# A depthwise convolution's banded tiles built in zeroed buffers, and an FFN weight ring split in two

## The chip, the cores and the metric

One core of a Trainium2 chip runs the program. The metric is the time of one execution on the device, in microseconds (us). Five engines work beside each other, each in its own fixed order of instructions: TensorE (PE, matmuls, with its weight loads as PEld), VectorE (DVE), ScalarE (ACT), GpSimd (POOL) and SyncE (SP). Transfers are issued from the queues of SP, ACT and POOL.

## The reference

One layer of a hybrid encoder block in float32: D = 1024, 2048 positions and 16 meta positions ahead of them.

```python
h = concatenate([meta, x])
z = rms_norm(h, norm_mix_g)
conv_v, conv_gate, ssm_u = split(z @ w_in)              # 512 channels each
u = conv_v * sigmoid(conv_gate)
y = depthwise_conv(u, conv_w, width=31, centred) + conv_b
conv_out = silu(layer_norm(y, ln_g, ln_b))
y5 = gelu(bidirectional_ssm(ssm_u) + d_skip * ssm_u)    # 32 groups of 16 channels
ssm_out = y5 * sigmoid(y5 @ glu_w + glu_b)
h = h + concatenate([conv_out, ssm_out]) @ w_out
z = rms_norm(h, norm_ffn_g)
h = h + square(relu(z @ w_ff1)) @ w_ff2                 # 4096 wide
return rms_norm(h, norm_final_g)[16:]
```

The change bears on `depthwise_conv` and on the buffers of the two big products behind it.

## The kernel before

Float32 products are made of three matmuls on a high and a low part (`mm3`, L158 to L160); `split` makes the parts, the high one by a cast on ACT (L141) and the low one by a subtraction on DVE (L142). A matmul of 512 columns follows the one ahead of it after 0.23 us. A scheduler sets each engine's order when the program is built; pools with rings of buffers put in the waits.

The stages around the change:

- **Parameters, near 90 us.** `conv_params` turns the 31 taps of each channel round, puts them into a row `wp` of 63 with zeros on both sides, and multiplies that row by an 8-channel diagonal to `ep`, [128, 504], which is stored in `edr[j]` in DRAM (j counts 128 channels).
- **Projections, to 496 us.** The gate and value products end with v(3,3). `stv` is value times gate; POOL stores it in `vdr` (L282). It is laid out so that 16 steps of time lie on one partition row.
- **Convolution, 496 to 595 us.** Sixteen calls of `conv_quad`, 32 channels each. A call loads `u8` (a piece of `vdr`), and for each of four groups of 8 channels a tile `cb` of 128 rows by 384 columns (16 steps x 8 channels, by 3 x 128): the tap of the right distance where row and column have the same channel, else 0. Three matmuls per group (L910, each in two records) with `u8` as the stationary operand sum into PSUM; four adds on DVE put the bias to it and write `cv[blk]`. The tiles `cb` lie in a ring of six, each filled by one transfer from `edr` with 128 runs of 1536 bytes (L908), 192 KB.
- **Beside and behind it.** `load_wout(0)` and `load_wout(1)` bring the two halves of w_out through three `raw4` buffers (L924) and split them to woh/wol. `s5_out(blk)` loads `y` (L958), makes GELU of it and splits the result to `ghl`, multiplies by the GLU weights (`glu`, from `gw`), and hands `mhl` to `wout_mm(0, blk, ...)` (`wo0_t`, products of w_out's lower half). `ln_out` normalises `cv` for `wout_mm(1, blk, ...)`. glu0 and wo0_0 to wo0_3 belong to block 0, glu1 and wo0_4 and so on to block 1.
- **Slots.** `zslot` gives out four large buffers, two with the tag za and two with zb. They held z, its blocks in turn, then w_out's halves, then FFN operands (zx1, zx6 in za; zx3, zx4 and every second chunk of hid and w2 in zb).
- **FFN, 840 us on.** Seven products per pair of 128-wide pieces (a Strassen step). `hid_pair` makes the weight operands 1, 2, 6, 7, 5, 3, 4 in that order, each a tile [128, 2, 4, 128] of a ring of nine with the tag w.

Of the kernel before, what the change touches and what calls it, by code (L numbers as in the profile page):

```python
# [37 lines left out]
def hymba_kernel(ctx, tc, x, meta, norm_mix_g, w_in, conv_w, conv_b, conv_ln_g, conv_ln_b,  # L38
# [70 lines left out]
    edr = [DR.tile([P, 504], F32, name=f"edr{j}") for j in range(4)]  # L109
# [52 lines left out]
    with ExitStack() as es2:  # L162
# [181 lines left out]
        with (tc.tile_pool(name="pp", bufs=1, reuse_waits="tile") as PP,  # L344
# [254 lines left out]
            def conv_params():  # L599
                cw = tp([31, 512], "cw", tag="cw", bufs=2)  # L600
                SP.dma_start(cw, conv_w[0])
                m8 = tp([P, 8], "m8")
                V.tensor_reduce(out=m8, in_=ident.rearrange("p (a c) -> p c a", c=8), axis=mybir.AxisListType.X,
                                op=ALU.add)
                for j in range(4):
# [5 lines left out]
                    ep = tp([P, 63, 8], f"ep{j}", tag="cw", bufs=2)  # L611
                    mul(ep, wp.unsqueeze(2).broadcast_to([P, 63, 8]), m8.unsqueeze(1).broadcast_to([P, 63, 8]))
                    SP.dma_start(edr[j], ep.rearrange("p i c -> p (i c)"))
# [204 lines left out]
        def z_open(half):  # L818
            for q in "12675":
                n = f"zx{q}_{half}"  # L820
                zx[q] = (zslot([P, 2, 4, 512], n, tag="za") if q in "16" else
                         PR.tile([P, 2, 4, 512], F32R, tag=f"zx{q}", name=n, bufs=1))
# [44 lines left out]
        def z_late(half):  # L867
            for q, src in zip("34", sdr[half]):
                n = f"zx{q}_{half}"
                zx[q] = zslot([P, 2, 4, 512], n, tag="zb")  # L870
# [9 lines left out]
        with tc.tile_pool(name="p3", bufs=1, reuse_waits="tile") as P3:  # L880
# [18 lines left out]
            def conv_quad(q):  # L899

                j = q // 4
                ps = ks_ps(f"cv{q}", [P, 4, NT, 8])
                u8 = t3([P, 4, W], f"u8_{q}", bufs=2, tag="u8", pool=P3R)
                SP.dma_start(u8, dap(vdr[j], (q % 4) * 32 * NT * W, [[W, P], [P * W, 4], [1, W]]))
                for i in range(4):
                    g8 = 4 * (q % 4) + i
                    cb = t3([P, 384], f"cb{q}_{i}", tag="cb", bufs=6, pool=P3R)
                    SP.dma_start(cb, dap(edr[j], g8 * 8 * 504, [[504, 8], [8, 16], [1, 384]]))  # L908
                    for m in range(3):
                        T.matmul(ps[:, i].rearrange("p t c -> p (t c)"), u8[:, i, 2 - m:2 - m + P], cb[:, ts(m, P)],  # L910
                                 start=(m == 0), stop=(m == 2))
                bv = convb[:, 32 * q:32 * q + 32].rearrange("p (i c) -> p i c", c=8).unsqueeze(2)
                for blk in range(4):
                    o = cv[blk][:, :, 32 * q:32 * q + 32].rearrange("p t (i c) -> p i t c", c=8)
                    add(o, ps[:, :, 4 * blk:4 * blk + 4, :], bv.broadcast_to([P, 4, 4, 8]))
# [3 lines left out]
            def load_wout(top):  # L919
                hi = zslot([P, 4, D], f"woh{top}")  # L920
                lo = zslot([P, 4, D], f"wol{top}")
# [121 lines left out]
    def hid_pair(p, half, P4, order, late=None):  # L1043
# [10 lines left out]
        def wsplit(q, src):  # L1054
            w[q] = P4.tile([P, 2, 4, P], F32R, tag="w", name=f"w{q}_{n}", bufs=9)
            split(w[q][:, 0], w[q][:, 1], src)
# [65 lines left out]
    def second(half, P5, chunks):  # L1122
        def bufs(c):
            if c % 2 == 0:
                return [zslot([P, 2, 2, D], f"{q}{half}_{c}", tag="zb") for q in ("hid", "w2")]
# [102 lines left out]
```

## Time and profile before

| | us |
|---|---|
| median of 3 runs (lowest, highest) | 2204.61 (2204.16, 2206.48) |
| the profiled execution, its own time | 2203.35 |
| its span in the profile | 2201.5 |
| PE busy | 2073.1 (94%) |
| DVE busy | 1541.0 (70%) |
| ACT, POOL busy | 710.4 (32%), 155.5 (7%) |
| mean granted clock of TensorE | 0.986 of full speed |

The profile shows one execution. Busy time is the union of an engine's instructions; in the rows further down, what stands in brackets or behind the bar as idle is time in which that engine stood still before the instruction, with what released it. The chain of waits goes back from the last instruction, step by step, to whatever released it. Matmuls overlap, so the length of one record (0.4 us) is more than the spacing.

### The profile page before, as it was taken

Reading aid. Unit: us, or ns where it says so; the run is one execution under the profiler, and the core shown is the slowest. Engines: PE = TensorE matmul, PEld = TensorE weight load, DVE = VectorE, ACT = ScalarE, POOL = GpSimd, SP = SyncE. Lnnn points to the kernel's source line nnn. Section 1 sums busy time; section 2 is a strip of 40 time slices with the busy share of each in tenths; the row PEclk is TensorE's granted clock in tenths of the full one; section 3 lists DMA queues with packets and bytes.
Section 4 is the critical chain, followed back from the end, with each engine's and each line's share of the span. In section 5 each row is a group of like instructions: output and inputs, shape, how many; then the busy total and the mean of one; then the engine's idle time right before and its main releaser. Section 6 shows DMA issues by size and latency. Waiting matters only on the chain.

```text
span 2201.5 us, 27237 instructions
## 1 busy us (share of the span) xinstructions
PE 2073.1 (94%) x10124; PEld 1688.7 (77%) x10124; DVE 1541.0 (70%) x2783; ACT 710.4 (32%) x1046; POOL 155.5 (7%) x240
## 2 busy tenths in 40 slices
PE   7989889896899989999999999997999999999997
PEld 5767777775687767888888888885888888888886
DVE  7866799952397388556658888868666656676767
ACT  5323222220134144444434222214444443121212
POOL 1031244500001110000000000000000000000000
PEclk9999999999999999999999999998999999999999
DMA  6245444336653566333335343434333335232322
GB/s 193 94 159 184 126 112 118 116 96 192 206 168 111 191 216 206 114 115 115 107 113 201 106 124 105 162 97 144 115 107 103 100 122 186 92 109 84 115 77 86
DMA packets 217997, 290.94 MB, mean 132 GB/s; under 512 B 22221, under 2 KB 164057, under 8 KB 217352
## 3 DMA queue, kind: packets, MB, share of 16 engines
q1 hardware_dynamic: 193512, 241.84, 35.1%
q10 hardware_dynamic: 23072, 43.10, 5.4%
q0 software_dynamic: 1280, 4.26, 0.5%
q8 instruction: 80, 1.31, 0.3%
q14 instruction: 53, 0.43, 0.1%
HBM read 206.40 MB, written 82.76 MB: 131 GB/s over the span
## 4 chain that ended last, share of the span: by engine, by line
PE 73%; DVE 11%; DMA 8%; issue 2%; ACT 1%; SPq 0%; ACTq 0%; POOL 0%; DVEq 0%; POOLq 0%
PE f L158 10%; PE f L160 10%; PE f L159 10%; PE ps L1085 9%; PE ps L1084 9%; PE ps L1083 9%; DMA cb<-edr 3%; PE wo L158 2%; PE wo L160 2%; PE wo L159 2%; DMA h<-hdr 1%; DVE zo L761 1%; DVE s L45 1%; DVE zo L760 1%; PE cv L910 1%
## 5 line engine op out<-in xcount | busy, mean ns | idle before, releaser
L45 DVE TENSOR_TENSOR acc<-acc,f 128x512 f32<-128x512 f32 x496 | 331.6, 684 | 140.2 <-PE f L160 139.6
L158 PE MATMUL f<-w,hid 128*128 128x512 f32 x1024 | 399.8, 390 | 0.5 <-DVE acc L45 0.3
L159 PE MATMUL f<-w,hid 128*128 128x512 f32 x1024 | 398.6, 389 | 0.0
L160 PE MATMUL f<-w,hid 128*128 128x512 f32 x1024 | 398.5, 389 | 0.0
L1083 PE MATMUL ps<-zx,w 128*128 128x512 f32 x896 | 353.9, 395 | 16.0 <-ACT w L141 16.0
L1085 PE MATMUL ps<-zx,w 128*128 128x512 f32 x896 | 353.7, 395 | 1.9 <-DVE w L142 1.9
L1084 PE MATMUL ps<-zx,w 128*128 128x512 f32 x896 | 354.1, 395 | 0.0
L158 PEld LDWEIGHTS f<-w,hid 128*128 128x128 f32 x1024 | 192.2, 188 | 42.2 <-DVE acc L45 2.9
L160 PEld LDWEIGHTS f<-w,hid 128*128 128x128 f32 x1024 | 192.2, 188 | 40.2
L159 PEld LDWEIGHTS f<-w,hid 128*128 128x128 f32 x1024 | 192.2, 188 | 39.6
L1083 PEld LDWEIGHTS ps<-zx,w 128*128 128x128 f32 x896 | 169.3, 189 | 56.8 <-ACT w L141 17.8
L1085 PEld LDWEIGHTS ps<-zx,w 128*128 128x128 f32 x896 | 169.4, 189 | 40.8 <-DVE w L142 2.2
L1084 PEld LDWEIGHTS ps<-zx,w 128*128 128x128 f32 x896 | 169.3, 189 | 38.6
L141 ACT CAST hid<-rawh 128x1024 fp32r<-128x1024 f32 x64 | 67.3, 1052 | 358.9 <-PE f L160 351.0
L142 DVE TENSOR_TENSOR w<-sm,w 128x512 fp32r<-128x512 f32 x128 | 87.5, 691 | 84.7 <-ACT w L141 84.7
L141 ACT CAST w<-sm 128x512 fp32r<-128x512 f32 x128 | 78.2, 618 | 158.5 <-PE ps L1085 146.6
L141 ACT CAST w<-r 128x512 fp32r<-128x512 f32 x96 | 58.8, 617 | 129.3 <-PE ps L1085 118.1
L141 ACT CAST w<-raww 128x1024 fp32r<-128x1024 f32 x64 | 67.2, 1051 | 90.5 <-DMA raww<-in_w_ff_dram 90.5
L142 DVE TENSOR_TENSOR hid<-rawh,hid 128x1024 fp32r<-128x1024 f32 x64 | 78.2, 1222 | 16.8 <-ACT hid L141 16.8
L142 DVE TENSOR_TENSOR w<-raww,w 128x1024 fp32r<-128x1024 f32 x64 | 78.1, 1220 | 10.9 <-ACT w L141 10.9
L910 PE MATMUL cv<-cb,u 128*128 128x128 f32 x384 | 60.7, 299 | 23.4 <-DMA cb<-edr 21.4
L910 PEld LDWEIGHTS cv<-cb,u 128*128 128x128 f32 x384 | 49.9, 199 | 38.1 <-issue 16.9
(301 smaller groups left out, 3373.7 us busy)
## 6 DMA issues: line engine op xcount, KB each, us to landing
r<-in_w_ff_dram SPq DMA_DIRECT2D x64, 512.0 KB
fdr<-hh ACTq DMA_DIRECT2D x64, 512.0 KB
rawh<-fdr SPq DMA_DIRECT2D x64, 512.0 KB
raww<-in_w_ff_dram SPq DMA_DIRECT2D x64, 512.0 KB
h<-hdr SPq DMA_DIRECT2D x32, 512.0 KB
cb<-edr SPq DMA_DIRECT2D x64, 192.0 KB
x<-in_x_dram SPq DMA_DIRECT2D x16, 512.0 KB
mt<-gdr SPq DMA_DIRECT2D x64, 128.0 KB
```

The source lines that it names most:

```text
L45: return V.tensor_tensor(out=o, in0=a, in1=b, op=op)
L141: S.copy(out=hi, in_=src)
L142: on.tensor_tensor(lo, src, hi.bitcast(F32), ALU.subtract)
L158: T.matmul(ps, lh, rh, start=first, stop=False)
L159: T.matmul(ps, lh, rl, start=False, stop=False)
L160: T.matmul(ps, ll, rh, start=False, stop=last)
L760: V.tensor_tensor_scan(zo[0:64, 2:4 * W + 2], f(rh)[0:64, :], f(zi)[0:64, :], 0.0, ALU.mult, ALU.add)
L761: V.tensor_tensor_scan(zo[64:128, 0:4 * W][:, ::-1], f(rh)[64:128, ::-1], f(zi)[64:128, ::-1], 0.0, ALU.mult, ALU.add)
L910: T.matmul(ps[:, i].rearrange("p t c -> p (t c)"), u8[:, i, 2 - m:2 - m + P], cb[:, ts(m, P)], start=(m == 0), stop=(m == 2))
L1083: T.matmul(ps[q], w[q][:, 0, k], z[:, 0, k, :], start=(k == 0), stop=False)
L1084: T.matmul(ps[q], w[q][:, 0, k], z[:, 1, k, :], start=False, stop=False)
L1085: T.matmul(ps[q], w[q][:, 1, k], z[:, 0, k, :], start=False, stop=(k == 3))
```

## The change

It has three parts.

1. The taps are stored as they are: `edr[j]` is [128, 63], and the multiplication by the diagonal goes.
2. `toeplitz(h)` makes one tile for two quads (eight groups of 8 channels), [128, 8, 8, 48]: 128 rows (16 steps of time for each of 8 channels) by 8 groups, 8 channels and 48 columns. Four tiles cb0 to cb3 lie in the z slots. Each is cleared once (DVE clears cb0 and cb2, POOL cb1 and cb3), and then only its diagonal blocks are filled: 8 transfers, one a channel, of 16 rows by 8 by 48, that is 128 runs of 192 bytes, 24 KB. For h from 4 on, cb0 and cb1 are filled anew in turn; what lies off the diagonal stays zero. The matmuls read 8 x 16 columns out of it with a stride of 48, PSUM has channel before time, and the adds turn that round. The ring of `cb` goes. w_out's halves and the FFN's tiles change between za and zb.
3. The ring of nine in `hid_pair` becomes one of six (products 1, 2, 6, 7) and one of three (5, 3, 4).

```diff
@@ -106,7 +106,7 @@
     ydr = [DR.tile([P, NT, P], F32, name=f"ydr{j}") for j in range(4)]
     kdr = [DR.tile([P, 4, NPK], F32, name=f"kdr{i}") for i in range(4)]
     gdr = [DR.tile([2, H, 34 * H], F32, name=f"gdr{b}") for b in range(16)]
-    edr = [DR.tile([P, 504], F32, name=f"edr{j}") for j in range(4)]
+    edr = [DR.tile([P, 63], F32, name=f"edr{j}") for j in range(4)]
     pdr = [DR.tile([P, D], F32, name=f"pdr{t}") for t in range(NT)]
     hdr = [DR.tile([P, D], F32, name=f"hdr{t}") for t in range(NT)]
     sdr = [[DR.tile([P, 4, 512], F32, name=f"sdr{half}_{q}") for q in range(2)] for half in range(2)]
@@ -599,18 +599,13 @@
             def conv_params():
                 cw = tp([31, 512], "cw", tag="cw", bufs=2)
                 SP.dma_start(cw, conv_w[0])
-                m8 = tp([P, 8], "m8")
-                V.tensor_reduce(out=m8, in_=ident.rearrange("p (a c) -> p c a", c=8), axis=mybir.AxisListType.X,
-                                op=ALU.add)
                 for j in range(4):
                     ps = tr_ps(f"tr_cw{j}")
                     T.transpose(ps[:, 0:31], cw[:, ts(j, P)], ident[0:31, 0:31])
                     wp = tp([P, 63], f"wp{j}", tag="wp", bufs=2)
                     GP.memset(wp, 0.0)
                     V.tensor_copy(wp[:, 16:47], ps[:, 0:31][:, ::-1])
-                    ep = tp([P, 63, 8], f"ep{j}", tag="cw", bufs=2)
-                    mul(ep, wp.unsqueeze(2).broadcast_to([P, 63, 8]), m8.unsqueeze(1).broadcast_to([P, 63, 8]))
-                    SP.dma_start(edr[j], ep.rearrange("p i c -> p (i c)"))
+                    SP.dma_start(edr[j], wp)
 
             z_block(0)
             z_tiles(0, 0, 2, lambda: SP.dma_start(gmix, norm_mix_g[0].partition_broadcast(P)))
@@ -818,7 +813,7 @@
         def z_open(half):
             for q in "12675":
                 n = f"zx{q}_{half}"
-                zx[q] = (zslot([P, 2, 4, 512], n, tag="za") if q in "16" else
+                zx[q] = (zslot([P, 2, 4, 512], n, tag="zb") if q in "16" else
                          PR.tile([P, 2, 4, 512], F32R, tag=f"zx{q}", name=n, bufs=1))
 
         def z_step(half, i, psa, psb, tmp):
@@ -867,7 +862,7 @@
         def z_late(half):
             for q, src in zip("34", sdr[half]):
                 n = f"zx{q}_{half}"
-                zx[q] = zslot([P, 2, 4, 512], n, tag="zb")
+                zx[q] = zslot([P, 2, 4, 512], n, tag="za")
                 for k in range(2):
                     r = (raw4 if k else lambda s_, n_: xx_tile(n_).rearrange("p (k n) -> p k n", k=2))(
                         [P, 2, 512], f"raw_{n}_{k}")
@@ -899,26 +894,38 @@
             def conv_quad(q):
 
                 j = q // 4
-                ps = ks_ps(f"cv{q}", [P, 4, NT, 8])
+                ps = ks_ps(f"cv{q}", [P, 4, 8, NT])
                 u8 = t3([P, 4, W], f"u8_{q}", bufs=2, tag="u8", pool=P3R)
                 SP.dma_start(u8, dap(vdr[j], (q % 4) * 32 * NT * W, [[W, P], [P * W, 4], [1, W]]))
+                cb = toeplitz(q // 2) if q % 2 == 0 else cbs[q // 2 if q < 8 else q // 2 % 2]
                 for i in range(4):
-                    g8 = 4 * (q % 4) + i
-                    cb = t3([P, 384], f"cb{q}_{i}", tag="cb", bufs=6, pool=P3R)
-                    SP.dma_start(cb, dap(edr[j], g8 * 8 * 504, [[504, 8], [8, 16], [1, 384]]))
                     for m in range(3):
-                        T.matmul(ps[:, i].rearrange("p t c -> p (t c)"), u8[:, i, 2 - m:2 - m + P], cb[:, ts(m, P)],
+                        T.matmul(ps[:, i], u8[:, i, 2 - m:2 - m + P], cb[:, 4 * (q % 2) + i, :, ts(m, 16)],
                                  start=(m == 0), stop=(m == 2))
                 bv = convb[:, 32 * q:32 * q + 32].rearrange("p (i c) -> p i c", c=8).unsqueeze(2)
                 for blk in range(4):
                     o = cv[blk][:, :, 32 * q:32 * q + 32].rearrange("p t (i c) -> p i t c", c=8)
-                    add(o, ps[:, :, 4 * blk:4 * blk + 4, :], bv.broadcast_to([P, 4, 4, 8]))
+                    add(o, ps[:, :, :, 4 * blk:4 * blk + 4].rearrange("p i c t -> p i t c"),
+                        bv.broadcast_to([P, 4, 4, 8]))
+
+            cbs = []
+
+            def toeplitz(h):
+
+                n = h if h < 4 else h % 2
+                if h < 4:
+                    cbs.append(zslot([P, 8, 8, 48], f"cb{h}", F32, tag="za" if h < 2 else "zb"))
+                    (GP if h % 2 else V).memset(cbs[h], 0.0)
+                for c in range(8):
+                    SP.dma_start(cbs[n][16 * c:16 * c + 16, :, c, :],
+                                 dap(edr[h // 2], (64 * (h % 2) + c) * 63, [[1, 16], [8 * 63, 8], [1, 48]]))
+                return cbs[n]
 
             wo = {}
 
             def load_wout(top):
-                hi = zslot([P, 4, D], f"woh{top}")
-                lo = zslot([P, 4, D], f"wol{top}")
+                hi = zslot([P, 4, D], f"woh{top}", tag="za" if top else "zb")
+                lo = zslot([P, 4, D], f"wol{top}", tag="za" if top else "zb")
                 for k in range(4):
                     r = raw4([P, D], f"raw_wo{top}_{k}")
                     SP.dma_start(r, w_out[0][(0 if top else 512) + k * P:(0 if top else 512) + (k + 1) * P, :])
@@ -1052,7 +1059,8 @@
         w = {}
 
         def wsplit(q, src):
-            w[q] = P4.tile([P, 2, 4, P], F32R, tag="w", name=f"w{q}_{n}", bufs=9)
+            tag, bufs = ("w", 6) if q in "1267" else ("wl", 3)
+            w[q] = P4.tile([P, 2, 4, P], F32R, tag=tag, name=f"w{q}_{n}", bufs=bufs)
             split(w[q][:, 0], w[q][:, 1], src)
 
         wsrc = {"1": (a11,), "6": (s2, (s1, a21, a22, ALU.add), (s2, s1, a11, ALU.subtract)),
@@ -1122,7 +1130,7 @@
     def second(half, P5, chunks):
         def bufs(c):
             if c % 2 == 0:
-                return [zslot([P, 2, 2, D], f"{q}{half}_{c}", tag="zb") for q in ("hid", "w2")]
+                return [zslot([P, 2, 2, D], f"{q}{half}_{c}", tag="za") for q in ("hid", "w2")]
             return [P5.tile([P, 2, 2, D], F32R, tag=q, name=f"{q}{half}_{c}", bufs=1) for q in ("hid", "w2")]
 
         first_two = [bufs(0), bufs(1)]
```

The scheduler moves instructions with it. Three places follow; in a row, what stands before the arrow is written, what stands behind it is read, and "waits" names the engines and queues waited for.

**DVE, ahead of conv's first adds.** Before:

```order
L45 TENSOR_TENSOR stv3_2_4633<-v3_2_4608,sg3_2_4606 128x4x128 [waits DMASW3_49,PE_49]
L142 TENSOR_TENSOR wol0_4968<-raw_wo0_0_4969,woh0_4967 128x1024 [waits DMAHW1_49,Activation_49]
L142 TENSOR_TENSOR wol0_4968<-raw_wo0_1_4973,woh0_4967 128x1024 [waits DMAHW2_49,Activation_49]
L45 TENSOR_TENSOR stv3_3_4690<-v3_3_4665,sg3_3_4663 128x4x128 [waits DMASW4_49,PE_49,Activation_49]
L142 TENSOR_TENSOR wol0_4968<-raw_wo0_2_4977,woh0_4967 128x1024 [waits DMAHW3_49,Activation_49]
L142 TENSOR_TENSOR gw0_4716<-raw_gw0_4714,gw0_4716 128x1024 [waits Activation_49]
L142 TENSOR_TENSOR gw1_4721<-raw_gw1_4719,gw1_4721 128x1024 [waits Activation_49]
L142 TENSOR_TENSOR wol0_4968<-raw_wo0_3_4981,woh0_4967 128x1024 [waits DMAHW4_49,Activation_49]
L45 TENSOR_TENSOR cv0_4710<-cv0_4724,convb_4708 128x4x4x8 [waits DMAHW5_49,PE_49]
```

Now:

```order
L918 MEMSET cb0_4717 128x3072 [waits PE_49]
L45 TENSOR_TENSOR stv3_2_4623<-v3_2_4598,sg3_2_4596 128x4x128 [waits DMASW3_49,PE_49]
L918 MEMSET cb2_4813 128x3072 [waits PE_49]
L45 TENSOR_TENSOR stv3_3_4680<-v3_3_4655,sg3_3_4653 128x4x128 [waits DMASW4_49,PE_49,Activation_49]
L142 TENSOR_TENSOR gw0_4706<-raw_gw0_4704,gw0_4706 128x1024 [waits Activation_49]
L142 TENSOR_TENSOR gw1_4711<-raw_gw1_4709,gw1_4711 128x1024 [waits DMASW6_49,DMASW7_49,DMASW5_49,Activation_49]
L45 TENSOR_TENSOR cv0_4700<-cv0_4714,convb_4698 128x4x4x8 [waits DMAHW7_49,PE_49]
```

The memset of cb2 stands ahead of stv3_3, and all four splits of wol0 have gone from here (they stand between quads 7 and 9 now).

**SP, at the end of conv.** Before, from the last cb tile on:

```order
L908 DMA cb15_3_5165<-edr3_112 128x1x384 [waits DMAHW6_49,PE_49]
L924 DMA raw_wo1_0_5176<-in_w_out_dram 128x1024 [waits DVE_49]
L924 DMA raw_wo1_1_5180<-in_w_out_dram 128x1024 [waits DMAHW7_49,DVE_49]
L924 DMA raw_wo1_2_5184<-in_w_out_dram 128x1024 [waits DMAHW0_49,DVE_49]
L958 DMA y1_0_5437<-ydr0_85 128x512 [waits DMAHW1_49,DVE_49]
L958 DMA y1_1_5448<-ydr1_86 128x512 [waits DMAHW2_49,DVE_49]
L924 DMA raw_wo1_3_5188<-in_w_out_dram 128x1024 [waits DMAHW6_49,DMAHW3_49,DVE_49]
L958 DMA y1_2_5459<-ydr2_87 128x512 [waits DMAHW4_49]
L958 DMA y1_3_5470<-ydr3_88 128x512 [waits DMAHW5_49,DVE_49]
L942 DMA pdr0_113<-xo0_0_5315 128x1024 [waits DVE_49]
```

Now, from the last u8 on:

```order
L899 DMA u8_15_5090<-vdr3_84 128x4x130 [waits DMAHW5_49,PE_49]
L931 DMA raw_wo1_0_5110<-in_w_out_dram 128x1024 [waits DMAHW6_49,DVE_49]
L931 DMA raw_wo1_1_5114<-in_w_out_dram 128x1024 [waits DMAHW7_49,DVE_49]
L931 DMA raw_wo1_2_5118<-in_w_out_dram 128x1024 [waits DMAHW0_49,DVE_49]
L949 DMA pdr0_113<-xo0_0_5249 128x1024 [waits DMAHW1_49,DVE_49]
L949 DMA pdr1_114<-xo0_1_5280 128x1024 [waits DMAHW2_49,DVE_49]
L949 DMA pdr2_115<-xo0_2_5310 128x1024 [waits DMAHW3_49,DVE_49]
L940 DMA xo0_3_5341<-in_x_dram 128x1024 [waits DMAHW4_49,DMAHW1_49]
L931 DMA raw_wo1_3_5122<-in_w_out_dram 128x1024 [waits DMAHW6_49,DMAHW5_49,DVE_49]
L965 DMA y1_0_5371<-ydr0_85 128x512
L965 DMA y1_1_5382<-ydr1_86 128x512 [waits DMAHW7_49]
L965 DMA y1_2_5393<-ydr2_87 128x512 [waits DMAHW0_49]
```

y1_0 and y1_1, which stood ahead of raw_wo1_3, stand behind it, and three stores of pdr and a load of xo have come ahead of both.

**PE, behind the last quad.** Before (nine glu0 and then all 96 matmuls of wo0_0 to wo0_3 follow):

```order
L910 MATMUL cv15_5147<-cb15_3_5165,u8_15_5148 128x128 [waits DMAHW5_49]
L910 MATMUL cv15_5147<-cb15_3_5165,u8_15_5148 128x128 x2
L158 MATMUL glu0_3_5296<-ghl0_1_5214,gw0_4716 128x512
L159 MATMUL glu0_3_5296<-ghl0_1_5214,gw0_4716 128x512
L160 MATMUL glu0_3_5296<-ghl0_1_5214,gw0_4716 128x512
L158 MATMUL glu0_3_5296<-ghl0_2_5225,gw1_4721 128x512
```

Now:

```order
L160 MATMUL wo0_3_5343<-woh0_4933,mhl0_2_5227 128x512
L158 MATMUL wo0_3_5343<-woh0_4933,mhl0_3_5246 128x512
L159 MATMUL wo0_3_5343<-wol0_4934,mhl0_3_5246 128x512
L160 MATMUL wo0_3_5343<-woh0_4933,mhl0_3_5246 128x512
L158 MATMUL glu1_0_5415<-ghl1_0_5379,gw0_4706 128x512 [waits Activation_49]
L158 MATMUL glu1_1_5434<-ghl1_0_5379,gw0_4706 128x512
L159 MATMUL glu1_0_5415<-ghl1_0_5379,gw0_4706 128x512 [waits DVE_49]
L160 MATMUL glu1_0_5415<-ghl1_0_5379,gw0_4706 128x512
L158 MATMUL glu1_0_5415<-ghl1_1_5390,gw0_4706 128x512 [waits Activation_49]
```

After cv15 only the last twelve matmuls of wo0_3 (the last four of them shown) stand ahead of glu1; the other 84 of wo0_0 to wo0_3 and all of glu0 stand between the quads.

## Rows read from the trace of the kernel before

**Rows 1.** The page: busy time by engine; the chain by engine and line.

```profile
PE 2073.1 (94%) x10124; PEld 1688.7 (77%) x10124; DVE 1541.0 (70%) x2783; ACT 710.4 (32%) x1046; POOL 155.5 (7%) x240
...
PE f L158 10%; PE f L160 10%; PE f L159 10%; PE ps L1085 9%; PE ps L1084 9%; PE ps L1083 9%; DMA cb<-edr 3%; PE wo L158 2%; PE wo L160 2%; PE wo L159 2%; DMA h<-hdr 1%; DVE zo L761 1%; DVE s L45 1%; DVE zo L760 1%; PE cv L910 1%
```

**Rows 2.** Windows: start:end us, length, busy us of PE, PEld, DVE, ACT, POOL, clock, DMA share, GB/s.

```profile
496.00:595.00 99.00, 72.39 (x434) 56.37 (x433) 24.51 (x77) 9.29 (x12) 0.54 (x1) 0.97 0.67 202
595.00:645.00 50.00, 50.00 (x223) 40.70 (x222) 49.44 (x115) 23.29 (x37) 0.00 (x0) 1.00 0.46 159
505.00:510.00 5.00, 3.42 (x16) 3.45 (x17) 0.17 (x1) 0.00 (x0) 0.00 (x0) 0.50 0.69 198
1513.00:1525.00 12.00, 1.22 (x2) 0.50 (x2) 11.79 (x39) 2.66 (x5) 0.00 (x0) 0.60 0.99 301
```

**Rows 3.** Groups by line: count, busy us, mean ns, idle before and releaser; conv's matmuls and adds.

```profile
L910 PE MATMUL cv<-cb,u 128*128 128x128 f32 x384 | 60.7, 299 | 23.4 <-DMA cb<-edr 21.4 <-DVE cv L45 0.7
...
L45 DVE TENSOR_TENSOR cv<-cv,convb 128x128 f32<-128x128 f32 x64 | 14.2, 284 | 67.8 <-PE cv L910 67.8
```

**Rows 4.** Chain of waits, 496 to 600 us: start us, length us, what.

```profile
500.72 5.73 DMA cb<-edr
...
584.66 7.64 DMA cb<-edr
...
593.29 0.23 PE glu L158
```

**Rows 5.** Groups of DVE, 80 to 100 us.

```profile
L45 DVE TENSOR_TENSOR ep<-wp,m 128x504 f32<-128x504 f32 x4 | 2.7, 681 | 1.6 <-DMA edr<-ep 0.9 <-PE tr_cw L607 0.7
```

**Rows 6.** Timeline: start us, length us, engine, operation; the start of conv on three engines.

```profile
496.45 0.69 DVE L45 TENSOR_TENSOR stv<-v,sg 128x512 f32<-128x512 f32 x1 [3.39 <-PE v L160]
...
497.68 0.54 POOL L282 DMA_DIRECT2D vdr<-stv  x1 [10.71 <-DVE stv L45]
...
506.58 5.46 PE L910 MATMUL cv<-cb,u 128*128 128x128 f32 x24 [4.84 <-DMA cb<-edr]
```

**Rows 7.** Groups of POOL, whole span: its memsets.

```profile
L700 POOL MEMSET bk<- 128x128 f32 x16 | 3.3, 206 | 65.3 <-PE k L706 65.3
...
L278 POOL MEMSET stu<- 128x4 f32 x16 | 1.5, 105 | 4.6 <-DMA udr<-stu 4.3 <-POOLq L1214 0.3
```

**Rows 8.** Line L674: duration ns min/median/max; and POOL's timeline at that time.

```profile
L674 DVE TENSOR_TENSOR pb<-pkb x16: 672/684/7112, 134.7 to 425.7; 128x512 f32<-128x512 f32 x16
...
140.57 0.72 POOL L675 TENSOR_TENSOR tab<-k1g,tab 128x260 f32<-128x260 f32 x1
```

**Rows 9.** DMA issues: KB each, median us to landing; and the chain at a load.

```profile
vdr<-stv POOLq DMA_DIRECT2D x16, 260.0 KB, 2.9
...
399.21 3.40 DMA u<-udr
```

**Rows 10.** Line L908: SP's issue of a cb tile, ns min/median/max.

```profile
L908 SPq DMA_DIRECT2D cb<-edr x64: 567/573/1017, 500.7 to 584.7; - x64
```

**Rows 11.** Timeline of SP, DVE and ACT, 585 to 618 us.

```profile
587.15 1.31 SPq L958 DMA_DIRECT2D y<-ydr  x2
...
605.25 0.66 DVE L987 BATCH_NORM_STATS2 st<-cv 128x6 f32<-128x512 f32 x1
...
617.46 0.62 ACT L141 CAST ghl<-y 128x512 fp32r<-128x512 f32 x1 [0.76 <-DVE y L45]
```

**Rows 12.** Timeline of SP and ACT, 461 to 467 us.

```profile
461.98 0.42 SPq L958 DMA_DIRECT2D y<-ydr  x1
...
466.84 1.15 ACT L960 ACTIVATE ga<-y 128x512 f32<-128x512 f32 x2 [2.53 <-DMA y<-ydr]
```

**Rows 13.** Timeline of PE, 628 us: the last matmul of glu1_3.

```profile
628.02 0.40 PE L160 MATMUL glu<-ghl,gw 128*128 128x512 f32 x1
```

**Rows 14.** The page's groups: first matmul of each FFN triple.

```profile
L1083 PE MATMUL ps<-zx,w 128*128 128x512 f32 x896 | 353.9, 395 | 16.0 <-ACT w L141 16.0
```

**Rows 15.** The page: queue 1, its packets, MB and share of 16 engines.

```profile
q1 hardware_dynamic: 193512, 241.84, 35.1%
```

## Prediction, made before the changed kernel ran

> **What bounds the kernel now.** I read the page first: PE is busy 94% of the span, and in the chain by line `DMA cb<-edr` is the only transfer with 3% [rows 1]. So a change pays only where PE stands idle, and the windows say where that is: in the conv stage, 496 to 595 us, PE is busy 72.4 of 99 us, and in the 50 us after it not idle at all [rows 2]. By groups, conv's matmuls work 60.7 us and PE idles 23.4 us ahead of them, 21.4 of it on the cb transfers [rows 3]. The chain of the stage reads: issue of a cb, 5.7 to 7.6 us until it is there, one or two us of matmuls, the next issue, since a quad's last tiles need ring slots that earlier matmuls free [rows 4]. So a quad takes (593.3 - 506.6)/16 = 5.4 us [rows 4, 6], where its 24 matmul records need 24 x 60.7/384 = 3.8 us [rows 3].
>
> All sums are against the profiled execution: span 2201.5, own time 2203.35, which is 1.3 us under the median of the runs, 2204.61. About 0.2% (4.4 us) is what a measurement can tell from no change here.
>
> **The taps, early.** Four multiplies of 0.68 us go from DVE [rows 5], and four stores shrink. Three of the four stand among parameter work that waits for other engines; I count one, the last, as standing in the way of what follows. Gain 0.6 us; bounds 0 and 2.7.
>
> **Start of conv.** Before, the last stv is multiplied at 496.45, its store leaves at 497.68, and conv starts at 506.58 [rows 6]. Now the first cb tiles are filled early (their memsets wait for block 2 of v only), but on DVE the memset of cb2 stands ahead of the last stv, and on POOL that of cb3 ahead of the last vdr store. A memset of 128x3072 is not in the trace. POOL clears 128x128 in 206 ns and 128x4 in 105 [rows 7]: 0.1 + 3068 x 0.101/124 = 2.6 us; for DVE I take 3.0. Bounds: 1.5, and 7, since a DVE operation that has a median of 0.68 us took 7.11 while POOL ran its own from 134.87 to 141.3 [rows 8]. So stv ends at 496.45 + 3.0 + 0.7 = 500.2; 0.5 us later, as in rows 6, the store leaves, and it lands 2.9 us after that [rows 9], at 503.7. u8_0 waits for it, since its buffer lies over the stage tile now, and 0.4 + 3.4 us on SP and the way (a load of the same size [rows 9]) make 507.5; with a semaphore or two conv starts at 507.7, 1.1 later than before. Behind u8_0 on SP stand u8_1 and the rest of cb1, which are wanted 4 us later.
>
> **The conv stage.** A part of a cb tile is 24 KB now and still 128 runs, as a whole one of 192 KB was; if runs set the price, it costs SP 0.573 us [rows 10]. For two quads that is 8 x 0.573 + 2 x 0.36 = 5.3 us of SP against 2 x 3.8 = 7.6 us of PE, so PE sets the pace; the bytes, 202 GB/s before [rows 2], fall eightfold. The adds read PSUM across rows: 284 ns each now; even doubled, 64 x 0.28 = 18 us more fit under the 67.8 us that DVE idles ahead of them [rows 3]. PE then runs 60.8 us of conv, 1.7 us more for the half clock at its start (24 records took 5.46 us and not 3.8 [rows 6], granted clock 0.50 [rows 2]), and between the quads 125 matmuls of glu0 and wo0 at 0.233 us [rows 4] = 29.2 us. 2.7 us of stalls stay: wo0's first low half is split on DVE behind quad 7's adds (2.2), and a refill may wait for the last reader of its tile (0.5). Conv ends at 507.7 + 60.8 + 1.7 + 29.2 + 2.7 = 602.1. Before, the same PE work was done at 593.3 + 93 x 0.233 = 615.0. **Gain 12.9 us** at this point; bounds 4 (memset at 7, stalls of 8) and 18 (memset at 1.5, no stall).
>
> **What is late next.** Before, the 96 wo0 matmuls (22.4 us) lay behind conv and covered the way from y1's loads to ghl1: those loads go out from 587.15, and ghl1's last cast is at 617.46 [rows 11]. Now 84 of the 96 are spent between the quads, and 12 are left, 2.8 us. And the way starts later: wol1 goes into cb1's slot, so DVE must do quad 15's adds and split wol1's first block (0.9 + 1.2 us) before SP may issue raw_wo1_3, whose third buffer that frees; y1's loads stand behind it. So y1_0 leaves 2.5 us past conv's end and is there at 2.5 + 4.9 = 7.4 (461.98 to 466.84 [rows 12]); square, scale, product, sigmoid, product and cast make 0.62 + 0.42 + 0.69 + 0.62 + 0.67 + 0.63 = 3.65, and one split of 1.2 stands ahead: ghl1_0 at 12.3. PE idles 12.3 - 2.8 = 9.5 us. The other three tiles follow some 2.9 us apart, of which DVE works 2.5, so glu1_0 and glu1_1 are done at 12.3 + 8.7 = 21.0 past conv's end, at 623.1. Before they were done at 628.4 - 24 x 0.233 = 622.8 [rows 13]. **The gain is given back whole**, and 0.3 us more. To this comes the clock: in the 12 us without matmuls at 1513 the granted clock is 0.60 [rows 2], and conv's start, after such a wait, paid 1.7 us; I take 1.7 again (bounds 0 and 2.5). And bn_stats of a block, 4 x 0.66 us, ran in this stretch [rows 11], where DVE is busy 49.4 of 50 us [rows 2]; they now stand behind the next block's ghl: 0 to 2.6, taken as 1.0.
>
> **Slots and FFN.** wo0, wo1, four zx tiles and the even hid/w2 change sides of the slot pairs; the last reader of each side is done where the old one was: 0, bounds -2 and 2. The ring of nine becomes six and three: a pair's last three products wait for the same three of the pair before, two products (2 x 2.8 us) later than they do now, of 19.4 us a pair. All PE idle time ahead of the first matmul of a product's triples is 16.0 us in the kernel [rows 14], most of it where a half begins, which hangs on other work. Cost 0, hidden by those products; bounds 0 and 3.
>
> **Sum:** 2203.35 - 0.6 + 0.3 + 1.7 + 1.0 = 2205.8 us (rounded up), 0.1% above the profiled execution and 0.05% above the median: nothing that can be told.
>
> **Rivals.** *(A) Faster: the way to ghl1 is shorter than I make it.* It hangs on conv's end, so each us by which conv ends earlier reaches the end of the kernel. With the memset at 1.5 and no stalls conv ends 4.2 us earlier; with ghl1's tiles at DVE's 2.5 us and y1 there in 3.6 instead of 4.9, glu1 is done 2.5 us earlier; a clock that stays up saves 1.7, and hidden bn_stats 1.0. Together 9.4: 2196.4, and with all four multiplies on the path 2194.3. For it: the queues carry less than in any row that I took. Against: four adds and four splits stand ahead on DVE.
>
> *(B) Slower: zeroing holds the last v.* If the two memsets stretch each other to 7 us as in rows 8, then stv, its store, u8_0 and all of conv come 4 us later, and PE has only seven glu0 matmuls there. With bn_stats in full (1.6 more) and the splits of wo0 holding cv adds for 2 us it is 2205.8 + 7.6 = 2213.4. It decides if the last stv starts after 501.5. Against it: a memset reads nothing.
>
> *(C) Slower: short runs fill the tile slowly.* Queue 1 spent 0.351 x 16 x 2201.5/193512 = 0.064 us on a packet [rows 15]; 128 on 16 engines are 0.5 us, within SP's 0.573. If a 192-byte run took twice the mean packet, 1.0 us a part, two quads would need 8.2 us against 7.6, and the stage 8 x 0.6 = 4.8 us more: 2210.6. The Trainium skill, "DMA: Bandwidth & Descriptors", section Specifications, speaks for C: it wants 512 B or more for line rate and has a read-modify-write below. By that rule the parts gain less than their bytes; no row of this trace shows how much.
>
> *(D) The tile is filled in time, but the matmuls run slower on it,* whose columns now stand 16 in a run. Each 10% costs 6 us; records over 0.158 us would show it.
>
> **Chances.** The forecast, within 0.2%, has 0.42; A 0.30; B 0.15, C 0.08 and D 0.05, together 0.28 for slower. The range reaches two us below A (2192) and to B (2214).
>
> **What would show it.** Right: the wait on `DMA cb<-edr` under 4 us in place of 21.4; conv's last matmul at 600 to 604; then 8 to 11 us of idle PE ahead of glu1_0, released by ACT's ghl cast, with a lower granted clock behind; FFN windows as long as before. Wrong: no such gap (A); a memset over 5 us and conv after 510 (B); cb waits at every second quad (C).

## The result and the profile after

The changed kernel took 2182.82 us (median of 4 runs, 2179.23 to 2187.8), beside 2204.39 us for the kernel before: a ratio of 0.9904, 95% interval 0.9882 to 0.9926. It is **faster by about 21 us, 1%**, outside the range of the prediction (2192 to 2214; 2205.8 was forecast, no change). The profiled execution took 2183.87 us, span 2182.1, that is 19.5 us less than the one of before.

The page of the changed kernel, busy time and chain by line, beside [rows 1]:

```profile
PE 2068.2 (95%) x10124; PEld 1694.4 (78%) x10124; DVE 1542.6 (71%) x2780; ACT 710.6 (33%) x1046; POOL 160.5 (7%) x242
...
PE f L158 10%; PE f L159 10%; PE f L160 10%; PE ps L1093 10%; PE ps L1092 10%; PE ps L1091 9%; PE wo L158 2%; PE cv L903 2%; PE wo L160 2%; PE wo L159 2%; DMA h<-hdr 1%; DVE zo L756 1%; DVE zo L755 1%; DMA u<-udr 1%; DVE s L45 1%
```

`DMA cb<-edr`, 3% before, is no longer among the lines of the chain. The groups of conv, beside [rows 3], and the new memsets:

```profile
L903 PE MATMUL cv<-cb,u 128*128 128x128 f32 x384 | 48.5, 289 | 1.5 <-DMA u<-vdr 1.1 <-DMA cb<-edr 0.4
...
L45 DVE TENSOR_TENSOR cv<-cv,convb 128x128 f32<-128x128 f32 x64 | 14.1, 284 | 35.6 <-PE cv L903 35.6
...
L918 POOL MEMSET cb<- 128x3072 f32 x2 | 5.3, 2662 | 16.2 <-PE v L160 16.2
L918 DVE MEMSET cb<- 128x3072 f32 x2 | 5.2, 2618 | 10.8 <-PE v L160 10.8
```

The idle time ahead of conv's matmuls is 1.5 us in place of 23.4, which was expected. Their busy time is 48.5 us in place of 60.7, which was not. The adds, which now read across PSUM rows, take the same 284 ns.

The windows, columns as in [rows 2]:

```profile
496.00:595.00 99.00, 81.78 (x519) 72.91 (x520) 40.03 (x96) 15.28 (x18) 2.88 (x2) 0.90 0.45 126
595.00:645.00 50.00, 47.10 (x190) 36.38 (x189) 49.08 (x140) 21.23 (x36) 0.00 (x0) 0.93 0.44 144
505.00:510.00 5.00, 4.82 (x24) 4.82 (x25) 0.00 (x0) 0.00 (x0) 0.00 (x0) 0.54 0.22 52
584.00:594.00 10.00, 1.31 (x10) 1.12 (x9) 6.04 (x11) 2.09 (x2) 0.00 (x0) 0.71 1.00 355
594.00:606.00 12.00, 9.68 (x24) 6.62 (x23) 11.61 (x28) 7.33 (x12) 0.00 (x0) 0.68 0.62 224
```

Behind conv PE stands still now, from 584.9 to 593.6, and in the 12 us from 594 on the mean granted clock is 0.68, between its two levels of 1.2 and 2.4 GHz.

Where the 19.5 us lie, by the same PE instructions in both traces: v's last matmul ends 0.7 us earlier (496.4, 495.6). From there to the last GLU matmul it is 187.8 us in place of 200.1, **12.3 less**. From there to the first FFN product it is 136.2 in place of 142.7, **6.5 less**. From the first FFN product on the two traces differ by under 0.3 us: the FFN ring gave nothing.

The 6.5 us are in no term of the prediction. In the kernel before, PE has this wait in that stretch (timeline of PE: start us, length us, the idle time ahead in brackets), and behind it, from 774 to 778, the mean granted clock is 0.58, near the lower level; from 764 to 770 it was 1.00:

```profile
774.03 0.81 PE L841 MATMUL trf<-ident,h 128*128 128x128 f32 x5 [4.17 <-DVE h L62]
774.63 0.80 PE L158 MATMUL wo<-woh,zc 128*128 128x512 f32 x1
```

In the changed kernel the wait is not there. So three questions were left to experiments: why conv's matmuls were cheaper, where the 6.5 us came from, and what holds PE behind conv.

### The profile page after: what moved, and what is told of

Its sections match the earlier page's. It is cut to its first block, busy times and chain, and to the rows that moved or that the text cites. A ratio compares the mean times of both kernels' runs of the same rounds, so it can differ in the third digit from the quotient of the medians.

```text
span 2182.1 us, 27333 instructions
## 1 busy us (share of the span) xinstructions
PE 2068.2 (95%) x10124; PEld 1694.4 (78%) x10124; DVE 1542.6 (71%) x2780; ACT 710.6 (33%) x1046; POOL 160.5 (7%) x242
## 4 chain that ended last, share of the span: by engine, by line
PE 76%; DVE 12%; DMA 4%; issue 3%; ACT 1%; SPq 0%; ACTq 0%; POOL 0%; DVEq 0%; POOLq 0%
PE f L158 10%; PE f L159 10%; PE f L160 10%; PE ps L1093 10%; PE ps L1092 10%; PE ps L1091 9%; PE wo L158 2%; PE cv L903 2%; PE wo L160 2%; PE wo L159 2%; DMA h<-hdr 1%; DVE zo L756 1%; DVE zo L755 1%; DMA u<-udr 1%; DVE s L45 1%
## 5 line engine op out<-in xcount | busy, mean ns | idle before, releaser
L45 DVE TENSOR_TENSOR hh<-c,ps 128x512 f32<-128x512 f32 x64 | 44.0, 688 | 48.6 <-PE ps L1093 47.5
L45 DVE TENSOR_TENSOR xo<-xo,wo 128x512 f32<-128x512 f32 x64 | 43.8, 684 | 46.6 <-PE wo L160 43.3
```

Source lines behind the costliest of these rows:

```text
L45: return V.tensor_tensor(out=o, in0=a, in1=b, op=op)
```

## Experiments

Lengths of stages in every run's profiled execution, in us, taken from the same PE instructions: (a) from the end of v to the end of conv, (b) to the end of the last GLU product, (c) to the first FFN product; (d) the wait ahead of the first transposes of h (`trf`; "none" is under 0.9); (e) the time from SP's issue of the last store of pdr to its next load of xo, which waits for that store. Columns a to e come from one execution each, the ratio from all. In (a) PE also does other matmuls, 40 before, 132 in the changed kernel, 25 in e6 and 16 in e5; those not done there are left to (b), so (a) and (b) are best read as a sum.

| run | a | b | c | d | e | ratio to before (95%) |
|---|---|---|---|---|---|---|
| before | 96.9 | 103.2 | 142.7 | 4.2 | 4.7 | 1 |
| e1 rings alone | 96.0 | 103.1 | 146.0 | 5.7 | 4.8 | 0.9998 (0.9988 to 1.0008) |
| e3 slots alone | 101.1 | 100.1 | 143.5 | 5.4 | 4.8 | 0.9995 (0.9984 to 1.0006) |
| e8 before, w_out later | 96.2 | 103.4 | 145.1 | 4.8 | 4.7 | 0.9996 (0.9987 to 1.0006) |
| e9 before, fetch shifted | 95.9 | 103.2 | 136.1 | none | 3.2 | 0.9969 (0.9957 to 0.9980) |
| changed kernel | 89.3 | 98.5 | 136.2 | none | 2.8 | 0.9904 (0.9882 to 0.9926) |
| e2 changed, one ring | 89.4 | 98.7 | 139.2 | 3.0 | 3.4 | 0.9903 (0.9888 to 0.9918) |
| e4 changed, DRAM places | 89.3 | 98.9 | 139.0 | 2.6 | 3.4 | 0.9904 (0.9889 to 0.9918) |
| e12 changed, fetch shifted | 89.2 | 98.5 | 138.4 | 1.5 | 3.1 | 0.9889 (0.9873 to 0.9906) |
| e7 changed, w_out later | 89.1 | 99.6 | 136.7 | none | 3.0 | 0.9915 (0.9898 to 0.9931) |
| e11 changed, stores on POOL | 88.7 | 97.5 | 137.4 | 1.2 | 3.3 | 0.9895 (0.9882 to 0.9909) |
| e10 e11 and w_out later | 89.0 | 92.4 | 139.2 | 2.0 | 3.2 | 0.9882 (0.9867 to 0.9897) |
| e6 dense tiles in slots | 91.2 | 106.6 | 137.7 | none | 2.9 | 0.9966 (0.9953 to 0.9979) |
| e5 no cb loads | 62.7 | 109.3 | 139.0 | none | 2.6 | 0.9858 (0.9843 to 0.9873) |

**e1: the rings alone.**

```diff
-            w[q] = P4.tile([P, 2, 4, P], F32R, tag="w", name=f"w{q}_{n}", bufs=9)
+            tag, bufs = ("w", 6) if q in "1267" else ("wl", 3)
+            w[q] = P4.tile([P, 2, 4, P], F32R, tag=tag, name=f"w{q}_{n}", bufs=bufs)
```

> The kernel before with only the FFN weight ring split into six and three. In the changed kernel's trace the first FFN product starts 19.6 us earlier than before and the last one 19.7 us earlier, so nothing was won inside the FFN. My theory: 0, within 2 us of the kernel before (2202 to 2207). Rival (the two rings bring the 6 us that the changed kernel wins between 750 and 775 us, by another placement of tiles): 2196 to 2200.

Measured: 2205.27 us beside 2207.02 for the kernel before. There is no change, as expected.

**e2: the changed kernel with one ring**, the same lines the other way round.

> The changed kernel with the FFN weight ring of nine put back. My theory: as the changed kernel, 2180 to 2186, about 20 us below the kernel before. Rival (the rings bring 6 us): 2187 to 2190.

Measured: 2185.58 us, the changed kernel's ratio. So the rings bring nothing.

**e3: the sides of the slots alone**, in the kernel before (the tags of woh/wol, zx1, zx6, zx3, zx4, hid and w2 as in the change).

> The kernel before with only the slot sides exchanged (w_out's halves and the FFN tiles between za and zb), conv untouched. My theory: 0, within 2 us of the kernel before, and the wait of 4.2 us ahead of the first transposes of h near 770 us is still there. Rival (the sides bring the 6 us between 750 and 775 us): 2196 to 2200, that wait gone.

Measured: 2205.6 us beside 2207.02, and the wait is there (5.4 us). So the sides of the slots bring nothing.

**e4: the old places in DRAM.**

```diff
+    epad = [DR.tile([P, 441], F32, name=f"epad{j}") for j in range(4)]
     pdr = [DR.tile([P, D], F32, name=f"pdr{t}") for t in range(NT)]
```

> The changed kernel, but with four unused tensors of 441 columns in DRAM behind the tap rows, so that all later DRAM buffers (pdr, hdr, sdr) lie where they lay before. Theory that the place in DRAM makes stores of 512 KB land in 2.6 to 3.8 us instead of 4.7 to 5.3: the 4.2 us wait near 756 us comes back, 2186 to 2192. Rival (place does not matter): as the changed kernel, 2180 to 2186.

Measured: 2185.18 us, the ratio of the changed kernel; the store (column e) keeps 3.4 us. So the place in DRAM does not decide it. With e2 it shows that (d) moves between none and 3 us among kernels whose PE program is the same, but not to the 4 to 6 us of the old convolution.

**e5: loads of cb for quad 0 only**, in the kernel before. The other 60 of 64 loads are left out, so the convolution is that of the wrong taps.

```diff
-                    cb = t3([P, 384], f"cb{q}_{i}", tag="cb", bufs=6, pool=P3R)
-                    SP.dma_start(cb, dap(edr[j], g8 * 8 * 504, [[504, 8], [8, 16], [1, 384]]))
+                    if q == 0:
+                        cbk.append(t3([P, 384], f"cb{q}_{i}", tag="cb", bufs=6, pool=P3R))
+                        SP.dma_start(cbk[i], dap(edr[j], g8 * 8 * 504, [[504, 8], [8, 16], [1, 384]]))
+                    cb = cbk[i]
```

> The kernel before, but the cb tiles are loaded for quad 0 only and all sixteen quads read these four (left out: 60 of 64 loads, so the convolution is that of the wrong taps). It shows conv with the old dense layout and no transfers to wait for. Theory that a matmul record costs 0.115 us wherever it stands in a long run (in the changed kernel 48 records take 5.52 us) and that the 0.158 us of before were start and end of short runs: 24 records in about 2.8 us, conv's work 44 to 46 us, total 2165 to 2174. Rival (the new layout makes the matmuls faster, the old one has 0.137 us a record, 12 in 1.8 us): 24 records in 3.3 us, 52 us, total 2174 to 2182.

Measured: 2172.84 us, ratio 0.9858. Conv's matmuls are busy for 46.9 us, a little over the 44 to 46 expected. Conv's timeline in the changed kernel (first line) and here, with the old dense columns (next two):

```profile
523.45 5.52 PE L903 MATMUL cv<-cb,u 128*128 128x128 f32 x48
```

```profile
531.25 5.83 PE L914 MATMUL cv<-cb,u 128*128 128x128 f32 x48 [0.25 <-DMA u<-vdr]
537.94 5.60 PE L914 MATMUL cv<-cb,u 128*128 128x128 f32 x48 [0.86 <-DMA u<-vdr]
```

48 records, two quads, take 5.52 to 5.83 us in both layouts: 0.115 to 0.12 us each, 2.8 us a quad. The new layout neither helps nor hurts. What made the records look like 0.158 us is the wait itself: in the kernel before they ran for the most part in pieces of six, each with its own start and its own last 0.27 us. Three rows of its timeline:

```profile
539.78 0.91 PE L910 MATMUL cv<-cb,u 128*128 128x128 f32 x6 [0.62 <-DMA cb<-edr]
540.85 0.94 PE L910 MATMUL cv<-cb,u 128*128 128x128 f32 x6 [0.17 <-DMA cb<-edr]
542.35 1.78 PE L910 MATMUL cv<-cb,u 128*128 128x128 f32 x12 [0.56 <-DMA cb<-edr]
```

A row of 12 is two such pieces; the short wait between them (0.19 us from start to start) is hidden under the last record. Within the pieces the records start 0.112 us apart at the median, in this trace, in that of the changed kernel and in that of e5.

**e6: dense tiles in the slots.** The change's slots and order, but each group's tile is filled with 192 KB from the taps times the diagonal, into [128, 8, 384], without memsets.

```diff
-                for c in range(8):
-                    SP.dma_start(cbs[n][16 * c:16 * c + 16, :, c, :],
-                                 dap(edr[h // 2], (64 * (h % 2) + c) * 63, [[1, 16], [8 * 63, 8], [1, 48]]))
+                for g in range(8):
+                    SP.dma_start(cbs[n][:, g, :], dap(edr[h // 2], (64 * (h % 2) + 8 * g) * 504, [[504, 8], [8, 16], [1, 384]]))
```

> The changed kernel with the slots, but each tile filled densely as before (taps times diagonal, 64 transfers of 192 KB, no zeroing, the old layout of columns). It tells the depth of the buffers (32 small tiles ahead in place of six) from the bytes. If depth and early filling do it: 2180 to 2190, like the changed kernel. If the bytes do it: 12.6 MB at about 200 GB/s are 63 us, of which half can be brought before conv; conv waits for the second half, ends 8 to 20 us later than in the changed kernel, 2190 to 2204.

Measured: 2196.92 us, ratio 0.9966. Its conv matmuls in the groups:

```profile
L908 PE MATMUL cv<-cb,u 128*128 128x128 f32 x384 | 53.6, 308 | 29.8 <-DMA u<-vdr 26.6 <-DMA y<-ydr 2.1 <-DVE gb L45 1.1
```

PE still idles 29.8 us, now ahead of u8, whose loads are issued among tiles of 192 KB; the first of these waits is 15.1 us. The total is what was expected if the bytes do it, by another way: counted from v's end, conv ends only 1.9 us later than in the changed kernel and not 8 to 20, but with 25 other matmuls done by then in place of 132, and (b) is 8.1 us longer. The deeper buffers alone don't do it: the eightfold fewer bytes do. Of the 10.0 us by which its profiled execution lies under that of before, 5.0 are in (c): 137.7 in place of 142.7.

**e7: w_out's second half later**, in the changed kernel.

```diff
-            load_wout(1)
             for blk in range(4):
                 s5_out(blk)
+                if blk == 1:
+                    load_wout(1)
```

> The changed kernel with load_wout(1) called after s5_out(1) in place of before s5_out(0): the loads of raw_wo1 stand behind y1's on SP. The changed kernel's PE waits 8.7 us for the add into xo0_3 (its load waits for a store of pdr that took 7.8 us beside the raw_wo1 loads) and 2.0 us for ghl1. My theory: stores and loads are quicker without 2 MB beside them and the gap falls to 3 to 5 us; 4 to 8 us less than the changed kernel, 2175 to 2180. Rival (the chain of adds on DVE and y1's own loads sets the gap): 2180 to 2186.

Measured: 2185.07 us, where 2175 to 2180 was expected. The wait for the add into xo0_3 fell from 8.7 to 3.7 us as expected, but the waits ahead of glu1 are 2.0 and 2.7 us (2.0 and 0.4 in the changed kernel), the mean granted clock is 0.70 from 585 to 600, and (b) is 99.6.

**e8: the same move in the kernel before.**

> The kernel before with the same move of load_wout(1). PE had no gap there before, so my theory is 0 (2202 to 2207); what e7 wins is then tied to the change. Rival (the move helps by itself, since DVE is full there): 2196 to 2201.

Measured: 2203.74 us beside 2203.89: no change, as expected.

**e9: twelve more transposes early.** By then ten traces were at hand. They fall into two sorts by column (e): 4.7 to 4.8 us in the four kernels whose convolution is as before (before, e1, e3, e8), 2.6 to 3.4 in the six others. Packets say why. The view of the transfers shows for a window the mean busy tenths of the 16 DMA engines in 40 slices, and by queue the packets, MB and share. Of the kernel before, first from the window 731:732, then from 733:735; the store was issued at 729.83:

```profile
q1 hardware_dynamic: 93, 0.34, 84.2%
q8 instruction: 1, 0.02, 6.7%
...
DMA  0010010010010010010000000000000000000000
...
q1 hardware_dynamic: 7, 0.02, 3.0%
```

A store of 512 KB has its 128 packets on 16 engines. One packet of queue 8 (instructions, 16 KB) came onto one of them in the midst, from 731.36 to 732.44, and that engine's last eight packets follow it one by one until 734.04; the other 15 engines were done at 732.1. The later loads of xo, counted from this store, go 2 to 4 us later than in the changed kernel, and that ends in the wait (d). The edit moves PE's instructions by 24, and nothing else:

```diff
+                    for _ in range(4):
-                    T.transpose(ps[:, 0:31], cw[:, ts(j, P)], ident[0:31, 0:31])
+                        T.transpose(ps[:, 0:31], cw[:, ts(j, P)], ident[0:31, 0:31])
```

> The kernel before, with each of the four transposes of the taps done four times (12 more weight loads and 12 more matmuls on PE near 85 us, where it has gaps; nothing else). In the four runs with the old convolution a 16 KB packet of queue 8 (instructions) falls at 730.8 to 731.4 us, across the store of pdr issued at 729.8, whose last packets on that DMA engine come 2 us late; the store lands after 4.7 us and every later store and load of xo follows late, until PE waits 4.2 to 5.7 us ahead of the first transposes of h. In the runs with the new one it falls at other times and the store takes 2.8 to 3.4 us. Theory (the fetch does it): 24 instructions more bring the fetch 2 to 3 us earlier, the store lands in under 3.5 us, that wait falls to 0 to 3 us, total 3 to 6 us under the kernel before (2198 to 2202 where that has 2204). Rival (the phase of the loop has another cause in the convolution's end): the wait stays 4 to 6 us, total as before.

Measured: 2198.32 us beside 2203.51, ratio 0.9969 (0.9957 to 0.9980): **the kernel before, with more work in it, is 0.3% faster.** The timeline of SP and PE here, with PE's first transposes of h, which wait for nothing now:

```profile
728.45 0.32 SPq L943 DMA_DIRECT2D pdr<-xo  x1
731.60 0.32 SPq L934 DMA_DIRECT2D xo<-pdr  x1
...
768.62 0.55 PE L842 MATMUL trf<-ident,h 128*128 128x128 f32 x3
```

The packet of queue 8, in the view of the transfers, lies ahead of the store now, in the window 727:728:

```profile
q8 instruction: 1, 0.02, 8.9%
```

In the kernel before, SP's two rows:

```profile
729.83 0.32 SPq L942 DMA_DIRECT2D pdr<-xo  x1
734.52 0.32 SPq L933 DMA_DIRECT2D xo<-pdr  x1
```

The packet starts 0.5 us ahead of the store's issue here, and 1.5 us behind it in the kernel before. Column (c) is 136.1, as in the changed kernel. The trace is that of the fastest of seven executions (2193.35 us), so the 5.2 us between the medians are the better measure of what the move is worth.

All 14 traces fit. The store's data move from 0.8 us after its issue on. Where the packet runs from 1.1 to 1.5 us after the issue until 2.6 or 2.7, (e) is 4.7 to 4.8 us (before, e1, e3, e8). Where it is over by 0.7 to 1.3 us after the issue, (e) is 2.8 to 3.4, longest in e2 and e4, where it ends last. Where it starts after 2.4 us (e5, e6), (e) is 2.6 and 2.9. The wait (d) goes with (e): 4.2 to 5.7 us where (e) is 4.7 or more, 2.6 to 3.0 where it is 3.4, none to 2.0 where it is 3.1 to 3.3, none below. So most of the 6.5 us are the packet's; how many depends on the execution, since (c) is 136.2 to 139.2 in the changed kernel and in e2 and e4, which have its PE program.

**e12: the same transposes in the changed kernel.**

> The changed kernel with the same twelve extra transposes. There the fetch already ends before the store's packets begin, so moving it earlier should win nothing. Theory: as the changed kernel, 2180 to 2186, no wait over 3 us ahead of the transposes of h. Rival (the transposes help by themselves, by the clock or by another order): 4 to 7 us under the changed kernel, 2175 to 2179.

Measured: 2180.63 us, inside what the theory gave; its interval (0.9873 to 0.9906) takes in the changed kernel's ratio. But the packet did not move: it starts 0.15 us ahead of the store's issue here and 0.20 in the changed kernel. So the run does not show what moving it is worth there. It shows that the transposes by themselves bring no clear gain, which speaks for the packet as the cause in e9, and that 24 instructions more do not always shift the packet.

**e11: the first three stores of pdr on POOL's queue**, in the changed kernel.

```diff
-                    SP.dma_start(dst[t], xx)
+                    (GP if top == 0 and t < 3 else SP).dma_start(dst[t], xx)
```

The run that the expectation calls the one before it is e10, further down.

> As the run before it, but load_wout(1) stays where it is: the stores alone move to POOL's queue. The wait of 8.7 us for the add into xo0_3 should go (xo0_3's load is issued right behind raw_wo1's three), but y1 still stands behind three raw_wo1 loads, and wol1 behind the last quad: the wait ahead of glu1 grows from 2 to 5 to 8 us. Theory (SP's order): 2178 to 2182. Rival (DVE): as the changed kernel, 2181 to 2185.

Measured: 2180.72 us, inside the theory's range and 0.3 us under its rival's, so the time does not tell them apart. By the trace the wait for xo0_3 fell to 3.1 us, where it was to go, and the one ahead of glu1 rose to 6.2, as expected.

**e10: both moves together** (e7's and e11's).

> The changed kernel with two moves: the first three stores of pdr go out from POOL's queue (idle there) in place of SP's, where they stand behind the last u8 loads; and load_wout(1) comes after s5_out(1). The next load of xo then waits for nothing on SP, and y1's loads stand right behind it. Theory (queue order on SP sets the 10.7 us of PE waits behind conv): waits of 1 to 4 us in all there, 5 to 9 us under the changed kernel, 2174 to 2178. Rival (DVE, busy 5.6 to 6.0 of 6 us there, sets it): waits of 7 to 10 us, at most 2 us under the changed kernel, 2180 to 2185.

Measured: 2178.39 us, ratio 0.9882 (0.9867 to 0.9897), the fastest kernel of the study that computes the whole, some 4.8 us under the changed kernel by the ratios, a little under the 5 I had set. The two intervals overlap, so by the total a gain is not shown; the stage (b) is 92.4 us in place of 98.5. In the profiled execution (c) takes 3.0 of these 6.1 us back, with a wait (d) of 2.0. Waits of over 0.9 us behind conv add up to 3.8 us in place of 10.7. DVE was busy 14.1 of 15 us there (585 to 600), so it was near its limit, but with SP's queue in another order most of the waits are gone: the order was what had made PE wait.

## Why the prediction was wrong

**Conv's start** was right in its mechanism and 1.9 us late: 507.7 forecast, from which the sum takes the early 0.6, so 507.1; measured 505.2. The memsets cost 2.62 and 2.66 us (3.0 and 2.6 forecast), and running at the same time neither held up the other, so the first step of rival B did not happen:

```profile
496.10 2.62 DVE L918 MEMSET cb<- 128x3072 f32 x1 [8.04 <-PE v L160]
498.63 0.63 DVE L45 TENSOR_TENSOR stv<-v,sg 128x512 f32<-128x512 f32 x1
```

The store, which left at 499.80, and the load of u8_0 took 2.3 and 2.9 us, where the rows that I had taken gave 2.9 and 3.4; they make up the rest of the difference.

**The step that failed** is "a quad takes ... where its 24 matmul records need 24 x 60.7/384 = 3.8 us". It divided the busy time of a group that stood in short pieces by its count. Measured: 48 records in 5.52 us, 2.76 a quad. The forecast had 60.8 + 1.7 us of conv; it was 48.5, two stretches at a lower clock among it (7.72 us for the first 48 records, 4.45 for the 24 behind the wait of 2.1 us). The 1.7 us for the half clock were counted twice besides: the 5.46 us of the first 24 records are part of the 60.7. With the stalls as forecast (2.1 ahead of wo0's low half, 0.4 for a refill), conv's end came at 584.9 and not at 602.1 - 0.6 = 601.5: 1.9 from the start, 62.5 - 48.5 = 14.0 from the records, 0.7 from the rest. The trace of before had the true rate, within its pieces (0.112 us from start to start) and in an undisturbed run of nearly the same kind: 16 records of the SSM's 130-column matmuls, with one start and one end among them, in 2.07 us, in the chain of waits:

```profile
235.03 2.07 PE v L742 x16
```

Less the last one's length of 0.27 us that is (2.07 - 0.27)/15 = 0.12 us from start to start.

**"The gain is given back whole"** fell with it, since the way to ghl1 hangs on conv's end and moved along. Its own size was about right: glu1_0 and glu1_1 were done at 615.7 - 24 x 0.233 = 610.1, 25.2 past conv's end, where 21.0 and 2.7 for clock and bn_stats were forecast. But the mechanism was another. I had PE waiting 9.5 us for ghl1 behind raw_wo1_3. It waited 8.7 us for the add into xo0_3:

```profile
593.59 0.79 PE L158 MATMUL wo<-woh,mhl 128*128 128x512 f32 x1 [8.69 <-DVE xo L45]
```

SP's timeline shows why that add was late. Three stores of pdr, whose data were there by 571.5, stood on SP behind the last u8 and three loads of raw_wo. The load of xo0_3 waits for the first of them, 7.84 us in the chain of waits, while the DMA engines were full (share 1.00, 355 GB/s in 584 to 594):

```profile
579.76 1.43 SPq L949 DMA_DIRECT2D pdr<-xo  x3
587.61 0.33 SPq L940 DMA_DIRECT2D xo<-in_x_dram  x1
588.04 0.37 SPq L931 DMA_DIRECT2D raw_wo<-in_w_out_dram  x1
588.47 2.63 SPq L965 DMA_DIRECT2D y<-ydr  x4
```

The chain there:

```profile
579.76 7.84 DMA pdr<-xo
587.61 5.15 DMA xo<-in_x_dram
```

The row order on SP that stands ahead of the prediction had these three stores in it, in front of xo0_3 and y1; the prediction read past them. e10 changed the places of the stores and of raw_wo's loads, and the waits behind conv fell from 10.7 to 3.8 us.

**The rest of the sum.** The early gain is 0.7 us (0.6 forecast), the FFN ring and the slots 0 (e1, e3). The 6.5 us in (c) were in no term and no rival: of the change only the slots' sides reach that stage, and e3 shows that they bring nothing; where the instruction packet falls does (e9). Forecast 2.4 us more than before, measured 19.5 less: of the 21.9 between, 1.9 are the start, 14.7 conv's length, 6.5 the stage (c), and 1.5 go the other way behind conv, which makes 21.6. That the 6.5 us came on top was luck; without them the total would still lie under the range.

**The rivals.** A had the right sign and, in "each us by which conv ends earlier reaches the end", the right mechanism; its size was too small for the same reason. C did not come: SP issues a part in 429 ns at the median (573 before, [rows 10]), and PE waited 0.4 us in all for parts, as the group of conv in the result shows.

```profile
L920 SPq DMA_DIRECT2D cb<-edr x64: 303/429/1503, 487.2 to 577.0; - x64
```

The Trainium skill, "DMA: Bandwidth & Descriptors", section Specifications, wants at least 512 B for line rate. This case's traces agree in the direction: a packet of 192 B took 16 ns on the mean in the changed kernel, one of 1536 B 73 ns in the kernel before, so by the byte the short one cost 1.75 times as much. But it took less than a quarter of the long one's time, where C had it at twice the mean packet of 64 ns, and no price reached PE. D did not come either (e5).

## What to carry to other kernels

Don't take a matmul's price from busy time over count where the group stands in short pieces between waits; look for the longest unbroken run of that shape, in any stage, and divide that. When a wait on a transfer goes, walk the queue that issued it row by row to the next wait, stores that have been ready for long among them. Here neither moving those stores to an idle queue (e11) nor moving the loads (e7) changed the time clearly; both together took 6.1 us from the stage (b). And where two traces differ in a stage that the edit doesn't touch, look at the packets before a story is made of it: here 24 instructions more on PE, with nothing else changed, moved the total of the kernel before by 0.3%.

## What the runs showed of the hardware

Instruction packets (16 KB, queue 8, 0.9 to 1.6 us each in the 14 traces beside this store) share the 16 DMA engines with data. One that fell into a 512 KB store made the time to the load that waits for it 4.7 to 4.8 us, in place of 2.6 to 3.4. That alone is about 2 us. It grew to a wait of 4 to 6 us on PE, and in the kernel before to 4 us at a mean granted clock of 0.58 behind it, since the loop of stores and loads stayed late. Why a loop once late stays late was not tried by itself. What places the packet is not shown either: 24 more instructions on PE moved it, counted from the store's issue, from 1.5 us behind to 0.5 us ahead in the kernel before (e9), and by 0.05 us in the changed one (e12).

Memsets of 128x3072 f32 took 2.62 us on DVE and 2.66 on POOL at the same time. Matmuls whose moving columns stand in runs of 16 with a stride of 48 cost what dense ones cost, 0.112 us from start to start.
